# Expert weights by expert in 8 KB pieces, and the final norm's vector by a broadcast transfer

## The chip, the cores and the metric

The kernel runs on one core of one Trainium2 chip. The metric is the device time of one execution in microseconds (us). The engines are TensorE (PE in the profile; PEld is its weight loads), VectorE (DVE), ScalarE (ACT), GpSimd (POOL) and SyncE (SP), which here does little else than issue transfers. Sixteen DMA engines move data from HBM into SBUF.

## The reference

One layer on 256 tokens of 1024 features, float32. Stick-breaking attention and multi-scale retention run side by side on projections of the normed input, their outputs are merged by sigmoid gates, projected and added to the input. Then comes a mixture of 16 small experts:

```python
for e in range(N_EXPERTS):
    hidden = jax.nn.silu(xt @ w_exp_gate[e]) * (xt @ w_exp_up[e])
    y = y + combine[:, e:e + 1] * (hidden @ w_exp_down[e])
...
return rms_norm(h, norm_final_g)
```

Here `xt` is the normed residual, `combine` has two nonzero weights for each token (the best two experts of the token's best group), and the gate, up and down weights of an expert are 1024x512, 1024x512 and 512x1024: 6 MB in float32, 96 MB for all sixteen. The result is normed once more, with the vector `norm_final_g` of 1024 values.

## The kernel before, in words

**Slots.** SBUF is cut into 27 slots of 1 MB (128 partitions of 8 KB). `take` takes the slot that has been free for longest, `give` returns one. A list of loads, made once, holds every weight tile of the kernel in the order of use, each 1 MB. `pump` (its transfers are issued in L163) walks this list: as long as there is a free slot and a limit allows it, it takes the slot and has SP issue the tile's transfers. The code is written out in one order per engine; SP executes its issues in that order, and each waits until the last reader of the slot's old content is through. So a tile's load is issued when a slot is returned in the code, and starts when that slot's last product has run.

**Dense part** (up to about 245 us): the input is split into two rounded parts, every projection is three products (L281, L282, L284 and L294), and attention and retention are woven in between. The first expert tiles are loaded meanwhile.

**Routing and gather.** Tokens are ranked per expert; each expert has 64 places (`CAP`). `gather` (its products are in L945) multiplies 128 feature columns of the token rows `hn`, as the stationary operand, with a one-hot matrix and so makes `xgt[:, c, :]`: 128 features on the partitions, the places of eight experts on the columns. Which 128 features stand in block `c` is said by `features(c2, c)`: every second column of a stretch of 256. The scale of the norm, `fp`, is packed in the same order (`pack`).

**Experts**, in pairs i = 0 to 7, the two experts of a pair on the two halves of the output partitions. For each pair there is a gate step, an up step (both `proj`, L996) and a down step (L1032). A step has four rounds r = 0 to 3, and each of them uses one tile of 1 MB:
- A gate or up tile r (`plan_rows`) holds rows 256r to 256r + 255 of both experts. Partition p has rows 2p and 2p + 1 of each expert, so there are two transfers of 512 KB, and each partition's piece is 4 KB in a row. Round r multiplies blocks c = 2r and 2r + 1 with it and returns its slot (`after`).
- A down tile (`plan_down`) holds 256 rows of one expert; partition p has rows p and 128 + p, two pieces of 4 KB, in one transfer. The very last tile comes in two transfers.
- Between up and down, `hidden` (L1016) transposes the product of both, 128 columns at a time, with the identity as the moving operand; the scatter (L1050) adds a pair's output to the four accumulators `F`.

The order of steps is g0, u0, then for each i: g(i+1), d(i), u(i+1), with two exceptions: d3 comes ahead of g4, behind the gather of the second eight experts, and d6 comes behind u7. The loads stand in the same order. Written out, up(2) is the step u2.

**Two slots of the experts' phase aren't for weights.** `after` takes one as a work buffer at the end of round 0 of u0, and another at the end of round 1 of u0. Each takes the slot that would have gone to the next load.

**Final norm.** `final_gain` is called twice, ahead of round 2 of the last up step. It makes the vector `norm_final_g`, spread over 128 partitions, by eight transposes of one parameter column each, widened to 128 columns (L1168), and two copies on ACT (L1169). By then every load stands in SP's order already. `finish` runs the last scatter, sums squares on ACT (L1185), multiplies by the vector on DVE (L1186, its first reader) and writes the result.

If an expert gets more than 64 tokens, a branch runs the experts again; it isn't taken here.

Of the kernel before, what the change touches and what calls it, by code (L numbers as in the profile page):

```python
# [13 lines left out]
AF = mybir.ActivationFunctionType  # L14
# [3 lines left out]
P = 128  # L18
T = 256
D = 1024  # L20
KC = D // P
NB = T // P
# [52 lines left out]
R_FG = 32  # L75
R_BR = 40
R_WR = 60
R_GN = 220
R_FP = 228
R_N = 236  # L80


def pack(ins):
    w = np.concatenate([ins["w_group_router"][0], ins["w_expert_router"][0]], axis=1)
    b = np.concatenate([ins["b_group_router"][0], ins["b_expert_router"][0]])
    return np.ascontiguousarray(np.concatenate([
        ins["norm_mix_g"][0].reshape(KC, P).T,
        ins["b_gate"][0].reshape(16, P).T,
        ins["ret_norm_g"][0].reshape(8, P).T,
        ins["norm_ffn_g"][0].reshape(8, P).T,  # L90
        np.broadcast_to(b[None, :], (P, 20)),
        w.reshape(KC, P, 20).transpose(1, 0, 2).reshape(P, 160),
        ins["norm_final_g"].reshape(8, P).T,
        ins["norm_ffn_g"][0].reshape(4, P, 2).transpose(1, 0, 2).reshape(P, 8),
    ], axis=1))


@with_exitstack
def layer(ctx: ExitStack, tc, cst, dec, prm, x, w_in, w_gate, w_sb_out, w_ret_out,
          w_out, w_exp_gate, w_exp_up, w_exp_down, out):  # L100
    nc = tc.nc
    pe, act, dve, pool, sp = nc.tensor, nc.scalar, nc.vector, nc.gpsimd, nc.sync
# [17 lines left out]
    def take(shape=(P, 2048), dt=F32):  # L120
        s = free.pop(0)
        uid[0] += 1
        t = big.tile(list(shape), dt, name=f"b{uid[0]}", tag=f"s{s}")
        held[id(t)] = (s, t)
        return t
# [5 lines left out]
    def small(shape, dt=F32, name=None, bufs=1, tag=None):  # L131
        uid[0] += 1
        return sm.tile(list(shape), dt, name=f"{name}_{uid[0]}", tag=tag or name, bufs=bufs)

    def bank(name="d", dt=F32):
        uid[0] += 1
        return pp[name].tile([P, 512 if dt == F32 else 1024], dt, name=f"p{uid[0]}", tag=name)
# [7 lines left out]
    raws = {}  # L145
# [5 lines left out]
    def rows(w, r0, nk, c0, n):  # L151
        return w[r0:r0 + nk * P, c0:c0 + n].rearrange("(kc p) n -> p kc n", p=P)

    def plan(key, shape, parts, hook=None):
        loads.append((key, shape, parts, hook))

    def pump():
        while loads and loaded[0] < limit[0] and free:
            key, shape, parts, hook = loads.pop(0)
            t = raws[key] = take(shape)  # L160
            loaded[0] += 1
            for i, (at, src) in enumerate(parts):
                sp.dma_start(t[at], src)  # L163
                if hook:
                    hook(i)
# [6 lines left out]
    def drop(key):  # L172
        give(raws.pop(key))


    par = small([P, R_N], F32, "par")
    act.dma_start(par, prm)
# [15 lines left out]
    ident = cw[:, 2048 - P:2048]  # L193
# [4 lines left out]
    ident = identr.bitcast(F32)  # L198
# [259 lines left out]

    def plan_rows(which, w, i):
        for r in range(4):  # L460
            e = [w[0, 2 * i + j][256 * r:256 * r + 256].rearrange("(p k) n -> p k n", k=2) for j in range(2)]
            plan((which, i, r), [P, 2, 2, 512], [((slice(None), j), e[j]) for j in range(2)])

    def plan_down(i):
        for r in range(4):
            e = rows(w_exp_down[0, 2 * i + r // 2], 256 * (r % 2), 2, 0, D)
            cut = (i, r) == (NP - 1, 3)
            plan(("d", i, r), [P, 2, D],
                 [((slice(None), k), e[:, k]) for k in range(2)] if cut else [(slice(None), e)])
# [11 lines left out]
    for which, i in STEPS:  # L481
        if which == "d":
            plan_down(i)
        else:
            plan_rows(which, w_exp_gate if which == "g" else w_exp_up, i)
# [3 lines left out]
    key, shape, parts, hook = loads[2]  # L489
# [253 lines left out]
    i = 0  # L743
# [138 lines left out]
    xgt = take([P, KC, T])  # L882
# [46 lines left out]

    fp = par[:, R_FP:R_FP + 8]  # L930
    cm = small([P, NB, NP, 3], F32, "cm")
    cmb = small([P, NB, NP, 3, 3], BF16, "cmb")
    y2, work, gs = [], {}, {}

    def features(c2, c):
        return slice(256 * c2 + c, 256 * c2 + 256, 2)

    def gather(k, pt, cs=range(4)):

        for c2 in cs:  # L940
            ps = bank("m").rearrange("p (c s) -> p c s", c=2)
            for tb in range(NB):
                for h in range(2):
                    for c in range(2):
                        pe.matmul(ps[:, c, :], hn[h][:, tb, features(c2, c)], pt[tb].rearrange("p e s -> p (e s)"),  # L945
                                  start=c == 0 and tb == 0 and h == 0, stop=c == 1 and tb == 1 and h == 1,
                                  skip_group_check=True)
            tt(xgt[:, 2 * c2:2 * c2 + 2, :], ps,
               fp[:, 2 * c2:2 * c2 + 2][:, :, None].to_broadcast([P, 2, 2 * P]), op=ALU.mult)
# [23 lines left out]

    def after(key):
        drop(key)
        if not work and key == ("u", 0, 0):
            w = take([P, 2048])
            work.update(b=w[:, 0:512], ht=[w[:, 512 + 512 * k:1024 + 512 * k].rearrange("p (f s) -> p f s", f=4)
                                           for k in range(2)],
                        pb=w[:, 1536:1664].bitcast(BF16))  # L980
        if not y2 and key == ("u", 0, 1):
            w = take([P, 2048], F32R)
            y2.append(w[:, 0:1024].rearrange("p (h n) -> p h n", h=2))
            work["S"] = [w[:, 1024 + T * k:1024 + T * k + T] for k in range(2)]
        pump()

    def proj(i, which, ps, hook):
        o = 64 * (i % 4)
        for r in range(4):
            if hook:  # L990
                hook(r)
            w = raws[(which, i, r)]
            for k in range(2):
                c = 2 * r + k
                for j in range(2):
                    pe.matmul(ps[64 * j:64 * j + 64, :], xgt[:, c, o:o + 64], w[:, j, k, :],  # L996
                              start=c == 0, stop=c == KC - 1)
            after((which, i, r))

    def gate(i, hook=None):  # L1000
        g = bank("g")
        proj(i, "g", g, hook)
        return g
# [4 lines left out]
    def up(i, hook=None):  # L1008
        u = bank("g")
        proj(i, "u", u, hook)  # L1010
        stt(work["b"], u, gs[i][:, 0:1], work["b"], op0=ALU.mult, op1=ALU.mult)  # L1011

    def hidden(i):
        hps = bank("m").rearrange("p (f s) -> p f s", f=4)
        for f in range(4):
            pe.transpose(hps[:, f, :], work["b"][:, f * P:(f + 1) * P], ident)  # L1016
        act.activation(work["ht"][i % 2], hps, AF.Copy)  # L1017

    def down(i, hook=None):

        ht = work["ht"][i % 2]
        ys = [(bank(b), cs) for b, cs in zip("gm", pieces(i))]
        for r in range(4):
            if hook:
                hook(r)
            w = raws[("d", i, r)]
            j = r // 2
            for y, cs in ys:
                for k in range(2):
                    f = 2 * (r % 2) + k  # L1030
                    for q in range(2):
                        pe.matmul(y[64 * q:64 * q + 64, cs], ht[:, f, 64 * j:64 * j + 64],  # L1032
                                  w[:, k, 512 * q + cs.start:512 * q + cs.stop],
                                  start=r == 0 and k == 0, stop=r == 3 and k == 1)
            after(("d", i, r))
        for y, cs in ys:
            hilo(y2[0][:, 0, cs], y2[0][:, 1, cs], y[:, cs])
# [107 lines left out]
    def tail():  # L1145
        i = NP - 1

        def in_first(r):
            if r == 2:
                hidden(i)  # L1150

        def in_second(r):
            if r == 1:
                scatter(i - 1)

        down(i - 1, in_first)
        down(i, in_second)

    final = []

    def final_gain(q):
        if len(final) < 2:
            if not final:
                final.append(take([P, 2048])[:, 0:D])
            ps = bank("m")
            for k in range(4):
                c = R_GN + 4 * q + k
                pe.transpose(ps[:, k * P:(k + 1) * P], par[:, c:c + 1].to_broadcast([P, P]), ident)  # L1168
            act.activation(final[0][:, 512 * q:512 * q + 512], ps, AF.Copy)  # L1169
            if q == 1:  # L1170
                final.append(take([P, NB, D]))

    halves = [slice(0, 512), slice(512, D)]

# [66 lines left out]
```

## Time and profile before

| | us |
|---|---|
| median of 3 runs (lowest, highest) | 460.0 (459.87, 460.77) |
| the profiled execution | 460.21 |
| its span, first to last instruction | 458.5 |
| PE busy | 440.3 (96%) |
| DVE busy | 186.7 (41%) |
| ACT busy | 166.7 (36%) |

The granted clock of TensorE was 0.994 of full speed. The profile counts 58037 DMA packets with 142.49 MB, 311 GB/s over the span. In its chain of work that ended last, PE has 90% and DMA 4%.

How to read it: times in all views are us from the span's start, those marked ns excepted. The slices cut the span into 40 parts of 11.46 us; a digit is the busy share in tenths. The chain is followed back from the last instruction, at each step to what released it. A wait for several semaphores is put down to the one that came last by the profile, and can belong to another. Ends of matmuls are modelled.

### The profile page before, as it was taken

How to read it: one execution, taken by the hardware profiler on the slowest of the kernel's cores; microseconds unless marked ns; L12 is line 12 of the kernel's file. 1: busy time of each engine (PE TensorE's matmuls, PEld its weight loads, DVE VectorE, ACT ScalarE, POOL GpSimd, SP SyncE). 2: the span in 40 equal slices, each digit the busy share in tenths (PEclk: the TensorE clock that was granted, in tenths of full speed). 3: DMA queues.
4: the chain of work that ended last, by engine and by line, in shares of the span. 5: the costliest groups of instructions: out<-in, count | busy, mean ns of one | idle time of the engine just before them, and what ended most of it. 6: DMA issues, size and time to landing. Idle time of an engine off the chain costs nothing.

```text
span 458.5 us, 6741 instructions
## 1 busy us (share of the span) xinstructions
PE 440.3 (96%) x2715; PEld 297.7 (65%) x2715; DVE 186.7 (41%) x349; ACT 166.7 (36%) x246; POOL 22.1 (5%) x36
## 2 busy tenths in 40 slices
PE   7899999999999999999999999999989999999991
PEld 6699878887899999999998433333343333333340
DVE  4756488654357865678646420101022010101003
ACT  3543687894663655344534021010100010101103
POOL 2400110100002200000001000000000000000000
PEclk9999999999999999999999999999999999999997
DMA  8999998239402179995958989999999999999972
GB/s 280 353 381 387 393 356 272 91 95 315 140 1 93 39 240 394 408 390 186 362 188 291 338 306 411 408 410 410 408 409 410 408 409 408 410 407 410 410 302 98
DMA packets 58037, 142.49 MB, mean 311 GB/s; under 512 B 3344, under 2 KB 23952, under 8 KB 57872
## 3 DMA queue, kind: packets, MB, share of 16 engines
q1 hardware_dynamic: 57568, 141.35, 82.5%
q10 hardware_dynamic: 432, 0.65, 0.4%
q8 instruction: 23, 0.38, 0.3%
q14 instruction: 14, 0.11, 0.1%
HBM read 140.93 MB, written 1.05 MB: 310 GB/s over the span
## 4 chain that ended last, share of the span: by engine, by line
PE 90%; DMA 4%; DVE 2%; ACT 1%; issue 1%; POOL 1%; SPq 0%; ACTq 0%; DVEq 0%
PE p L996 25%; PE p L294 20%; PE p L1032 9%; PE p L281 8%; PE p L284 8%; PE p L282 8%; DMA b<-in_w_exp_down 3%; PE p L945 2%; PE p L1050 2%; PE z L586 1%; DMA b<-in_x 1%; PE p L1016 1%; PE p L688 1%; PE p L629 1%; PE z L617 1%
## 5 line engine op out<-in xcount | busy, mean ns | idle before, releaser
L253 DVE TENSOR_TENSOR b<-b,b 128x1024 fp32r<-128x1024 f32 x72 | 88.7, 1240 | 71.8 <-ACT b L251 70.7
L996 PE MATMUL p<-b,b 128*64 128x512 f32 x512 | 115.1, 596 | 0.0
L294 PE MATMUL p<-b,b 128*128 128x512 f32 (+1 forms) x504 | 102.4, 359 | 1.1 <-ACT b L251 0.9
L251 ACT ACTIVATE b<-b 128x1024 fp32r<-128x1024 f32 x72 | 75.5, 1056 | 76.7 <-PE p L282 47.8
L294 PEld LDWEIGHTS p<-b,b 128*128 128x128 f32 x504 | 82.3, 189 | 15.2 <-ACT b L251 1.3
L996 PEld LDWEIGHTS p<-b,b 128*64 128x64 f32 x512 | 35.1, 137 | 66.6 <-issue 63.8
L281 PE MATMUL p<-b,b 128*128 128x256 f32 x288 | 71.6, 286 | 0.0
L282 PE MATMUL p<-b,b 128*128 128x256 f32 x288 | 70.8, 283 | 0.0
L1032 PE MATMUL p<-b,b 128*64 128x512 f32 (+1 forms) x288 | 57.5, 547 | 0.9 <-ACT b L572 0.7
L281 PEld LDWEIGHTS p<-b,b 128*128 128x128 f32 x288 | 55.2, 192 | 0.5
L282 PEld LDWEIGHTS p<-b,b 128*128 128x128 f32 x288 | 55.2, 192 | 0.0
L1032 PEld LDWEIGHTS p<-b,b 128*64 128x64 f32 x288 | 20.2, 137 | 36.0 <-issue 31.5
L284 PE MATMUL p<-b,b 128*128 128x256 f32 x288 | 41.1, 283 | 0.0
L573 DVE SCALAR_TENSOR_TENSOR b<-p,b 128x512 fp32r<-128x512 f32 (+1 forms) x13 | 7.3, 565 | 81.0 <-ACT b L572 81.0
L284 PEld LDWEIGHTS p<-b,b 128*128 128x128 f32 x288 | 37.5, 192 | 0.0
L1011 DVE SCALAR_TENSOR_TENSOR b<-p,share,b 128x512 f32<-128x512 f32 x8 | 6.0, 751 | 60.3 <-PE p L996 60.3
L972 ACT ACTIVATE b<-p 128x256 fp32r<-128x256 bf16 x8 | 3.1, 383 | 75.5 <-PE p L971 75.5
L572 ACT ACTIVATE b<-p 128x512 fp32r<-128x512 f32 (+1 forms) x13 | 6.4, 495 | 52.9 <-PE p L1032 52.2
L1006 ACT ACTIVATE b<-p,share 128x512 f32<-128x512 f32 x8 | 5.5, 687 | 21.2 <-PE p L996 21.2
L1017 ACT ACTIVATE b<-p 128x512 f32<-128x512 f32 x8 | 4.8, 597 | 20.7 <-PE p L1016 20.7
L945 PEld LDWEIGHTS p<-pt,b 128*128 128x128 f32 x64 | 8.1, 195 | 4.4 <-DVE pt L863 2.3
L1188 POOL TENSOR_TENSOR rf<-rf,mhalf 128x1 f32<-128x1 f32 x2 | 1.1, 540 | 203.4 <-DVE rf L1187 203.4
(169 smaller groups left out, 329.4 us busy)
## 6 DMA issues: line engine op xcount, KB each, us to landing
b<-in_w_exp_gate SPq DMA_DIRECT2D x64, 512.0 KB, 10.2
b<-in_w_exp_up SPq DMA_DIRECT2D x64, 512.0 KB, 10.2
b<-in_w_exp_down SPq DMA_DIRECT2D x31, 1024.0 KB, 12.7
b<-in_w_in SPq DMA_DIRECT2D x17, 1024.0 KB, 14.3
b<-in_w_gate SPq DMA_DIRECT2D x8, 1024.0 KB, 10.4
b<-in_w_ret_out SPq DMA_DIRECT2D x4, 1024.0 KB, 8.7
b<-in_w_out SPq DMA_DIRECT2D x4, 1024.0 KB, 6.4
b<-in_w_sb_out SPq DMA_DIRECT2D x2, 1024.0 KB, 5.1
```

The lines of the kernel that those rows point to most:

```text
L251: act.activation(hi, raw, AF.Copy)
L253: tt(lo, raw, hi.bitcast(F32), op=ALU.subtract)
L281: pe.matmul(ps, wh[:, k, cs], h[:, k, :], start=k == 0, stop=False)
L282: pe.matmul(ps, wh[:, k, cs], l[:, k, :], start=False, stop=False)
L284: pe.matmul(ps, wl[:, k, cs], h[:, k, :], start=False, stop=k == nk - 1)
L294: pe.matmul(ps[tb], kth(a, k)[:, tb * P:(tb + 1) * P], b[:, j, :], start=n == 0 and k == 0, stop=n == 2 and k == KC - 1)
L572: act.activation(hi, src, AF.Copy)
L573: stt(lo, src, 1.0, hi.bitcast(F32), op0=ALU.mult, op1=ALU.subtract)
L945: pe.matmul(ps[:, c, :], hn[h][:, tb, features(c2, c)], pt[tb].rearrange("p e s -> p (e s)"), start=c == 0 and tb == 0 and h == 0, stop=c ...
L996: pe.matmul(ps[64 * j:64 * j + 64, :], xgt[:, c, o:o + 64], w[:, j, k, :], start=c == 0, stop=c == KC - 1)
L1032: pe.matmul(y[64 * q:64 * q + 64, cs], ht[:, f, 64 * j:64 * j + 64], w[:, k, 512 * q + cs.start:512 * q + cs.stop], start=r == 0 and k == ...
L1050: pe.matmul(F[q][tb][:, cs], work["S"][i % 2][r, tb * P:(tb + 1) * P], y2[0][r, h, cs], start=False, stop=last and h == 1 and cs.stop == 5 ...
```

## The change

Four things:
- A gate or up tile holds 512 rows of one expert instead of 256 rows of both: tile r has expert r % 2, rows 512 (r // 2) on, partition p rows 4p to 4p + 3. It is one transfer of 1 MB with 8 KB in a row for each partition. Rounds 0 and 1 each read both of the first two tiles, rounds 2 and 3 both of the last two, and the slots are returned two at a time, behind rounds 1 and 3.
- A down tile has rows 2p and 2p + 1 on partition p, 8 KB in a row. The very last still comes in two transfers, of 4 KB pieces.
- The order of features follows: block c takes every fourth column of a stretch of 512 (`features`), `fp` is packed for it, and `hidden` transposes every second column of a stretch of 256.
- `final_gain` takes a slot and has SP issue one transfer that reads the vector's 4 KB for each of 128 partitions; the eight transposes and two copies go, and so do eight columns of the parameter table. The work buffer is taken at the end of round 3 of g0.

```diff
--- before.py
+++ after.py
@@ -75,9 +75,8 @@
 R_FG = 32
 R_BR = 40
 R_WR = 60
-R_GN = 220
-R_FP = 228
-R_N = 236
+R_FP = 220
+R_N = 228
 
 
 def pack(ins):
@@ -90,13 +89,12 @@
         ins["norm_ffn_g"][0].reshape(8, P).T,
         np.broadcast_to(b[None, :], (P, 20)),
         w.reshape(KC, P, 20).transpose(1, 0, 2).reshape(P, 160),
-        ins["norm_final_g"].reshape(8, P).T,
-        ins["norm_ffn_g"][0].reshape(4, P, 2).transpose(1, 0, 2).reshape(P, 8),
+        ins["norm_ffn_g"][0].reshape(2, P, 4).transpose(1, 0, 2).reshape(P, 8),
     ], axis=1))
 
 
 @with_exitstack
-def layer(ctx: ExitStack, tc, cst, dec, prm, x, w_in, w_gate, w_sb_out, w_ret_out,
+def layer(ctx: ExitStack, tc, cst, dec, prm, gfr, x, w_in, w_gate, w_sb_out, w_ret_out,
           w_out, w_exp_gate, w_exp_up, w_exp_down, out):
     nc = tc.nc
     pe, act, dve, pool, sp = nc.tensor, nc.scalar, nc.vector, nc.gpsimd, nc.sync
@@ -458,12 +456,12 @@
 
     def plan_rows(which, w, i):
         for r in range(4):
-            e = [w[0, 2 * i + j][256 * r:256 * r + 256].rearrange("(p k) n -> p k n", k=2) for j in range(2)]
-            plan((which, i, r), [P, 2, 2, 512], [((slice(None), j), e[j]) for j in range(2)])
+            e = w[0, 2 * i + r % 2][512 * (r // 2):512 * (r // 2) + 512].rearrange("(p k) n -> p k n", k=4)
+            plan((which, i, r), [P, 4, 512], [(slice(None), e)])
 
     def plan_down(i):
         for r in range(4):
-            e = rows(w_exp_down[0, 2 * i + r // 2], 256 * (r % 2), 2, 0, D)
+            e = w_exp_down[0, 2 * i + r // 2][256 * (r % 2):256 * (r % 2) + 256].rearrange("(p k) n -> p k n", k=2)
             cut = (i, r) == (NP - 1, 3)
             plan(("d", i, r), [P, 2, D],
                  [((slice(None), k), e[:, k]) for k in range(2)] if cut else [(slice(None), e)])
@@ -933,7 +931,7 @@
     y2, work, gs = [], {}, {}
 
     def features(c2, c):
-        return slice(256 * c2 + c, 256 * c2 + 256, 2)
+        return slice(512 * (c2 // 2) + 2 * (c2 % 2) + c, 512 * (c2 // 2) + 512, 4)
 
     def gather(k, pt, cs=range(4)):
 
@@ -973,7 +971,7 @@
 
     def after(key):
         drop(key)
-        if not work and key == ("u", 0, 0):
+        if not work and key == ("g", 0, 3):
             w = take([P, 2048])
             work.update(b=w[:, 0:512], ht=[w[:, 512 + 512 * k:1024 + 512 * k].rearrange("p (f s) -> p f s", f=4)
                                            for k in range(2)],
@@ -989,13 +987,15 @@
         for r in range(4):
             if hook:
                 hook(r)
-            w = raws[(which, i, r)]
+            w = [raws[(which, i, r // 2 * 2 + j)] for j in range(2)]
             for k in range(2):
                 c = 2 * r + k
                 for j in range(2):
-                    pe.matmul(ps[64 * j:64 * j + 64, :], xgt[:, c, o:o + 64], w[:, j, k, :],
+                    pe.matmul(ps[64 * j:64 * j + 64, :], xgt[:, c, o:o + 64], w[j][:, c % 4, :],
                               start=c == 0, stop=c == KC - 1)
-            after((which, i, r))
+            if r % 2:
+                after((which, i, r - 1))
+                after((which, i, r))
 
     def gate(i, hook=None):
         g = bank("g")
@@ -1013,7 +1013,8 @@
     def hidden(i):
         hps = bank("m").rearrange("p (f s) -> p f s", f=4)
         for f in range(4):
-            pe.transpose(hps[:, f, :], work["b"][:, f * P:(f + 1) * P], ident)
+            o = 256 * (f // 2) + f % 2
+            pe.transpose(hps[:, f, :], work["b"][:, o:256 * (f // 2) + 256:2], ident)
         act.activation(work["ht"][i % 2], hps, AF.Copy)
 
     def down(i, hook=None):
@@ -1159,16 +1160,11 @@
     final = []
 
     def final_gain(q):
-        if len(final) < 2:
-            if not final:
-                final.append(take([P, 2048])[:, 0:D])
-            ps = bank("m")
-            for k in range(4):
-                c = R_GN + 4 * q + k
-                pe.transpose(ps[:, k * P:(k + 1) * P], par[:, c:c + 1].to_broadcast([P, P]), ident)
-            act.activation(final[0][:, 512 * q:512 * q + 512], ps, AF.Copy)
-            if q == 1:
-                final.append(take([P, NB, D]))
+        if not final:
+            final.append(take([P, 2048])[:, 0:D])
+            sp.dma_start(final[0], gfr.to_broadcast([P, D]))
+        elif len(final) < 2:
+            final.append(take([P, NB, D]))
 
     halves = [slice(0, 512), slice(512, D)]
 
@@ -1228,7 +1224,7 @@
 
     ins = {k: np.ascontiguousarray(v) for k, v in inputs.items()}
     cst, dec = constants()
-    feed = {"cst": cst, "dec": dec, "prm": pack(ins)}
+    feed = {"cst": cst, "dec": dec, "prm": pack(ins), "gfr": ins["norm_final_g"].reshape(1, D)}
     feed.update({f"in_{k}": ins[k] for k in _INS})
     nc = _bacc.Bacc("TRN2", target_bir_lowering=False, num_devices=1, dynamic_dma_scratch_size=1024)
     args = [nc.dram_tensor(k, a.shape, mybir.dt.from_np(a.dtype), kind="ExternalInput").ap()
```

## Rows read from the trace of the kernel before

**Rows 1.** The slices of the page: PE, DMA, and what DMA moved.
```profile
PE   7899999999999999999999999999989999999991
...
DMA  8999998239402179995958989999999999999972
GB/s 280 353 381 387 393 356 272 91 95 315 140 1 93 39 240 394 408 390 186 362 188 291 338 306 411 408 410 410 408 409 410 408 409 408 410 407 410 410 302 98
```

**Rows 2.** The chain that ended last, 427 to 459: start, length, what.
```profile
430.02 15.67 DMA b<-in_w_exp_down
...
445.73 1.51 PE p L1032 x12
```

**Rows 3.** Waits, 429 to 448: engine, line, releaser, us in total, times, longest.
```profile
PEld p L1032 <- DMA b<-in_w_exp_down: 2.0, 3, 0.9
PE p L1032 <- ACT b L572: 0.7, 1, 0.7
```

**Rows 4.** The chain, 276 to 430.
```profile
277.43 6.87 PE p L1032 x32
...
371.22 0.66 PE p L1016 x4
...
408.84 1.13 PE p L1050 x8
...
425.06 1.02 PE p L1168 x8
426.08 3.61 PE p L996 x16
```

**Rows 5.** Windows: stretch, length, engines' busy time, clock, DMA share, GB/s last.
```profile
40.00:44.00 4.00, 4.00 (x36) 4.00 (x35) 1.97 (x3) 1.74 (x2) 0.00 (x0) 1.00 1.05 385
45.00:50.00 5.00, 5.00 (x32) 4.07 (x32) 2.13 (x4) 2.17 (x3) 0.00 (x0) 1.00 1.04 406
264.00:268.00 4.00, 4.00 (x24) 1.32 (x22) 0.81 (x5) 2.16 (x3) 0.00 (x0) 1.00 0.68 266
268.00:276.00 8.00, 7.87 (x44) 2.72 (x42) 1.62 (x6) 1.17 (x3) 0.00 (x0) 1.00 0.91 331
280.00:435.00 155.00, 152.87 (x761) 55.73 (x756) 18.08 (x49) 15.27 (x27) 0.00 (x0) 1.00 1.03 409
```

**Rows 6.** Waits of SP's queue, 262 to 275.
```profile
SPq L163 <- PE p L996: 7.6, 3, 5.9
```

**Rows 7.** Timeline of SP, single issues: start, length, line, what.
```profile
267.68 0.34 SPq L163 DMA_DIRECT2D b<-in_w_exp_up  x1
...
269.40 0.33 SPq L163 DMA_DIRECT2D b<-in_w_exp_up  x1
...
415.08 0.33 SPq L163 DMA_DIRECT2D b<-in_w_exp_up  x1
```

**Rows 8.** The chain, 249 to 275: rounds of up(0) and gate(1).
```profile
261.92 3.58 PE p L996 x16
...
265.77 7.02 PE p L996 x32
```

**Rows 9.** DMA, 45 to 50: packets by size.
```profile
DMA packets 641, 2.03 MB, mean 406 GB/s; under 512 B 32, under 2 KB 32, under 8 KB 514
```

**Rows 10.** DMA issues, 405 to 416: count, KB each, median us to landing.
```profile
b<-in_w_exp_up SPq DMA_DIRECT2D x8, 512.0 KB, 10.5
```

**Rows 11.** Timeline of DVE, 445 to 452: the vector's first reader.
```profile
449.33 0.69 DVE L1186 TENSOR_TENSOR b<-p,b 128x512 f32<-128x512 f32 x1 [1.19 <-ACT b L1185]
```

**Rows 12.** Weight loads by line, 245 to 459 (L281: 20:45): busy us, mean ns.
```profile
L996 PEld LDWEIGHTS p<-b,b 128*64 128x64 f32 x512 | 35.1, 137 | 66.6 <-issue 63.8 <-DMA b<-in_w_exp_gate 0.9 <-DMA b<-in_w_exp_up 0.7
...
L945 PEld LDWEIGHTS p<-pt,b 128*128 128x128 f32 x64 | 8.1, 195 | 4.4 <-DVE pt L863 2.3 <-issue 1.6 <-DVE b L948 0.5
...
L1016 PEld LDWEIGHTS p<-identr,b 128*128 128x128 f32 x32 | 3.4, 141 | 2.6 <-DVE share L965 1.8 <-issue 0.8
...
L281 PEld LDWEIGHTS p<-b,b 128*128 128x128 f32 x64 | 12.3, 192 | 0.0
```

## The prediction

> **What bounds the kernel now.** I read the slices first [rows 1]: TensorE (PE) is full nearly throughout, and from slice 25 to slice 38 the DMA engines are full too, at about 410 GB/s. So two chains run side by side through the experts, and only the end says which one sets the time. The chain that ended last [rows 2] says it: the last piece of the last down tile lands 15.67 us after its issue, at 445.69; the last 12 products start at 445.73, run 1.51 us, and the scatter and the final norm follow, which depend on nothing else. The waits of that stretch [rows 3] show PE's weight loads held three times by down tiles, 2.0 us in all, and 0.7 us put down to ScalarE. It is the only weight transfer on this chain from 405 on.
>
> So the expert loads are the bound, but only just. PE's own pace for what stands behind the last up products (they end at 426.08 + 3.61 = 429.69 [rows 4]): 6.87 us for a down step (x32), 0.66 for the hidden transposes, another 6.87 (the last step has twice the products at half the width), 1.13 for a scatter [rows 4]: 15.53, so PE alone would be through at 445.2; it was through at 445.73 + 1.51 = 447.24 [rows 2]. The 2.04 us between agree with the 2.0 of [rows 3].
>
> Where the load chain begins is seen in the windows [rows 5]: 409 GB/s from 280 to 435, but 266 and 331 from 264 to 268 and 268 to 276. There SyncE (SP) waits for PE to free a slot [rows 6]: 7.6 us in three waits. From about 276 on it has always something queued. The end of the loads is thus the moment at which the first load behind that idle stretch is issued, plus the service time of all behind it.
>
> **Pairs (later frees).** Before, each product round r of a gate or up step frees its tile. Now rounds 0 and 1 read the same two tiles and free them together at the end of round 1; 2 and 3 likewise. The first load behind the idle stretch is the first tile of up(2). Its slot now is that of up(0)'s third tile, free when round 2 of up(0) ended: issue 267.68 [rows 7]. After the change this slot is free when round 3 ends; the trace has an issue at that moment, the next one, 269.40. That is 1.72 us later. The tile before it (fourth of down(1)) moves too, to the end of round 1 of up(0), 261.92 + 3.58 = 265.50 [rows 8]; 3.9 us ahead of that issue, more than its own 2.5 us of transfer, so it doesn't push on. Later pairs matter less: gate(1)'s first pair is free at 265.77 + 7.02 = 272.79 [rows 8], before up(2)'s first two tiles are through. From 268 to 276 DMA lost 8 x (409 - 331)/409 = 1.5 us, of which some 1.1 lies ahead of up(2)'s data; the other 0.4 is regained, since both loads of a pair are then queued. Bounds: 1.3 (all regained) to 2.3 (a 1 MB transfer starts 0.5 later than a half one). I take **+1.8 us** on the end of the loads.
>
> **8 KB packets.** Behind up(2)'s first tile come 67 tiles of 1 MB; at 409 GB/s [rows 5] each takes 1.0486/0.409 = 2.564 us. How fast are 8 KB packets? In 40 to 44 the loads are of 2 KB and run at 385; at 16 engines that is 85.1 ns a packet, and 4 KB at 409 is 160.2 ns: 75.1 ns per further 2 KB. By this line 8 KB take 310.4 ns, or 422 GB/s. The trace has such packets: of the 641 between 45 and 50, 514 are under 8 KB, so 127 are of 8 KB (the table of decays, 1.04 MB) [rows 9]. The stretch moved 406 x 5 = 2030 KB; the other 990 at 385 take 2.57 us, the 1040 KB took 2.43: 427 GB/s. Bounds: 409 (no gain) and 427 (2.456 us a tile, 7.2 us over 67 tiles). I take 420, below the line: 2.497 us, 0.066 a tile, **-4.4 us**. With +1.8 the last tile lands 2.6 us earlier, at 443.1, and the products behind it end at 447.24 - 2.6 = 444.64.
>
> The Trainium skill (DMA: Bandwidth & Descriptors, "Why small descriptors are slow (HBM only)") gives three bus cycles per packet beside one for every 32 bytes: 131 cycles for 4 KB, 259 for 8. That is only 1.1% a byte; the line through 385 and 409 gives 3.2%. By the page the loads would gain some 2 us, not 4.4.
>
> **One transfer a tile.** Eight 512 KB transfers took 10.5 us to land [rows 10], at 409 GB/s about 8 x 0.524 MB: eight are in flight. Eight of 1 MB only deepen the queue: 0. SP issues half as many. That a round needs two tiles: the last half of up(7) was issued at 415.08 [rows 7] and landed near 425.6; round 2 began at 426.08. Now, with most of the 2.6 us gained, it lands near 423.5 and PE is there at 425.06, 1.5 us later: 0. If the loads were late here, PE would only wait sooner for what it waits for anyway.
>
> **The final norm's vector.** Eight products with the identity and their gap go: 1.02 us of PE at 425.06 [rows 4]. Its copies on ScalarE are off the path. This is hidden in the forecast: PE alone would end at 445.2 - 1.02 = 444.2, and the loads let it end at 444.64. It becomes the floor: no gain is over 447.24 - 444.2 = 3.04 us. If the 0.7 us wait on ScalarE in [rows 3] is real and no masked load, the floor is 444.9 and the gain 2.34. In its place 512 KB come on SP's queue, issued behind the last weights, so they delay none: 1.28 us at 409, there at 444.4. Its first reader is VectorE at 449.33 [rows 11], then 446.7: 2.3 us to spare. Bounds: 0, and 128 packets one after another at 160 ns, since all read the same 4 KB: 20.5 us. I take 0, as the stream in front of it has the same packet size and count per engine.
>
> **Strides.** The gather's 64 weight loads now step over 16 bytes, not 8; the 32 hidden transposes step over 8, not 4. The 8-byte step cost nothing so far: 195 ns against 192 for contiguous columns [rows 12]. A 16-byte step no row shows. Bounds: 0, and twice the column time: 128 columns take 195, 64 take 137 [rows 12], so 116 ns per load, 7.4 us in all. The transposes load at 141; at most 195 - 141 = 54 ns each, 1.7 us. I take 0 for both, by the row for the 8-byte step. The work buffer taken at the end of gate(0), and a parameter table of 8 columns less: 0; the one is first written a round later, the other is read long after it lands.
>
> **Sum.** Span 458.5, 460.21 with what lies around it: 460.21 - 2.6 = 457.6. The runs' median is 460.0, 0.2 lower, so I forecast **457.5**.
>
> **Rivals.**
> *A, bytes alone count.* The rate stays 409; then only the pairs' +1.8 is left: 462.0, slower. For it: 409 is held flat for 155 us, as at a ceiling. Against: 427 in the stretch with 8 KB. It decides if the gain per tile is under 1.8/67 = 0.027 us (413 GB/s).
> *B, half the gain.* Rows of 2 and 4 KB don't say how a third size goes; at 414 GB/s, half of what 420 gives, 2.2 us stand against 1.8: 459.8, no change that can be measured (a measurement of this kernel tells 0.2%, or 0.9 us, from none). For it: 385 and 409 are near each other, and the next doubling can only give less. Against: 427. The skill's packet cost above comes out here.
> *C, the 16-byte step.* If each of the 64 loads takes 116 ns more, half of it (3.7 us) comes ahead of up(0)'s frees and moves the loads as well, and PE's own end is 444.2 + 7.4 = 451.6: 460.2 + 4.4 = 464.6. It decides from 0.45 us on, where PE's own pace takes over. For it: no row has the step. Against: the step from 4 to 8 bytes shows no trend. The Trainium skill (SBUF — State Buffer, the note "SBUF cachelines" under "Door 1") has lines of 16 bytes and asks for at least two hits in one for full rate; an 8-byte step has two, in agreement with the 195 ns, a 16-byte step has one.
> *D, the vector comes late.* If 128 reads of one row run one after another it lands at 463.6, 16.9 us after its reader: 474.5; at half of that cost about 464. It decides from 3.6 us on (146 GB/s).
>
> **Chances.** Forecast 0.64 (its own range 456.9 to 459.0, by the floor and by 415 GB/s), A 0.08, B 0.12, C 0.10, D 0.06. Range: 456.9 to 462.1, with A and B in it. Faster by over 0.2% 0.66 (the forecast, and a weak D), within 0.2% 0.15 (B, and a weak C), slower 0.19.
>
> **What the next profile would show.** DMA at 418 to 425 GB/s from 280 on (409: A). Idle DMA near 265 to 271, up(2)'s first issue at about 269.4, and the last landing near 443.1. The gather's weight loads at 195 ns and its x16 at 2.19 us (C: over 250 ns and 4 us). The broadcast landing before 446. Waits for down tiles at the end of about 0.5 us instead of 2.0. I am wrong if the rate is up and the end is not earlier, or if PE waits for gate or up tiles.

## The result and the profile after

The changed kernel takes 465.58 us (median of 4 runs, 465.14 to 466.62) beside 460.25 for the kernel before on the same chip: a ratio of 1.0113, 95% interval 1.0101 to 1.0126. It is 5.3 us slower, where 2.5 us faster was forecast (457.5 from a median of 460.0), and the time lies outside the range of 456.9 to 462.1. The profiled execution took 465.14 us, its span is 463.3.

The slices first, of what DMA did (they answer to [rows 1]):

```profile
DMA  8999998249202289995948579999999999999942
GB/s 276 353 382 391 390 355 258 85 140 314 88 1 92 93 250 420 417 351 185 362 142 328 194 306 419 424 419 424 419 422 423 421 420 420 422 424 417 422 182 96
```

The transfers are faster than before in every full slice, at about 421 GB/s. Seen from the end of the kernel they are also through earlier: the last slice but one shows 182 GB/s instead of 302. The windows of the changed kernel (columns as in [rows 5]) say the same of the rate, and show DMA part idle ahead of it:

```profile
256.00:264.00 8.00, 8.00 (x37) 4.31 (x36) 3.71 (x16) 0.00 (x0) 0.00 (x0) 1.00 0.47 187
264.00:272.00 8.00, 8.00 (x40) 2.58 (x38) 0.97 (x5) 2.35 (x3) 0.00 (x0) 1.00 0.79 288
...
280.00:440.00 160.00, 158.14 (x760) 60.36 (x756) 18.09 (x49) 14.29 (x25) 0.00 (x0) 0.99 1.01 421
```

SP's issues around that stretch, and the last load's issue with its time to landing (answering to [rows 7]):

```profile
268.82 0.33 SPq L161 DMA_DIRECT2D b<-in_w_exp_down  x1
...
272.67 0.33 SPq L161 DMA_DIRECT2D b<-in_w_exp_up  x1
...
428.55 0.33 SPq L161 DMA_DIRECT2D b<-in_w_exp_down  x1
```
```profile
L161 SPq DMA_DIRECT2D b<-in_w_exp_down x1: 328/328/328, 428.6 to 428.6; - x1
...
DMA to landing us min/median/max: 17.4/17.4/17.4
```

The first load of up(2) is issued at 272.67, not at the forecast 269.4, and yet the last weights have landed at 428.55 + 17.4 = 445.95, hardly later than the 445.69 of [rows 2]. The end of the kernel is no longer theirs. The chain at the end (answering to [rows 2]):

```profile
436.13 3.43 PE p L1033 x16
439.57 0.68 PE p L1017 x4
...
446.69 5.33 PE p L1033 x48
452.02 1.37 PE p L1051 x14
```

It is PE without a gap; no wait for a down tile is left of the 2.0 us in [rows 3]. The products behind the last load end at 452.02 instead of 447.24: 4.78 us later, which is the span's 4.8. So PE lost time further up. The place is the gather. The chain of the changed kernel there, and then the weight loads by line (they answer to [rows 12]) and the products by line (busy us, mean ns):

```profile
249.07 4.01 PE p L943 x16
253.08 1.87 PE p L994 x8
254.95 2.07 PE p L943 x8
...
343.38 4.12 PE p L943 x16
```
```profile
L943 PEld LDWEIGHTS p<-pt,b 128*128 128x128 f32 x64 | 15.4, 329 | 4.3 <-DVE pt L861 2.3 <-issue 1.6 <-DVE b L946 0.3
...
L1017 PEld LDWEIGHTS p<-identr,b 128*128 128x128 f32 x32 | 4.7, 209 | 2.6 <-DVE share L963 1.8 <-issue 0.8
```
```profile
L943 PE MATMUL p<-pt,b 128*128 128x256 f32 x64 | 16.5, 412 | 1.3 <-DVE pt L861 1.2
...
L1017 PE MATMUL p<-identr,b 128*128 128x128 f32 x32 | 6.3, 322 | 0.8
```

And the gather's products in the kernel before:

```profile
L945 PE MATMUL p<-pt,b 128*128 128x256 f32 x64 | 9.1, 291 | 1.6 <-DVE pt L863 1.2 <-DVE b L948 0.3
```

A weight load of the gather takes 329 ns instead of 195, and its 64 products hold PE for 16.5 us instead of 9.1: 7.4 us. Half of it lies ahead of up(0), whose rounds free the slots, so up(2)'s first issue comes 272.67 - 267.68 = 5.0 us later: 1.7 by the pairs, 3.6 by the first half of the gather, less the 0.34 by which the gather began earlier (249.07, before 249.41).

The sum of PE's side: its own end was 445.2; 7.4 for the gather, 0.6 for the hidden transposes (0.74 instead of 0.66 for each of eight), less 1.02 for the products that went, less the 0.34 of the gather's start: 451.8, against 452.02 in the trace.

The granted clock of TensorE is lower as well, 0.988 of full speed over the run instead of 0.994. One stretch of that lies in the second gather. After 1.2 us of idling and some 2.6 us of the gather's products the clock fell from 1.00 to 0.50, its 1.2 GHz level, from 346 to 348, and was 0.65 from 348 to 350. This is not where the time went: the second gather's products took 4.12 + 3.96 = 8.08 us on the chain, the first's, at 1.00, took 4.01 + 2.07 + 2.07 = 8.15. Only the four transposes between them took 0.85 instead of 0.74.

### The profile page after: what moved, and what is told of

It reads as the page before. It is cut to its first block, busy times and chain, and to the rows that moved or that the text cites. A ratio compares the mean times of both kernels' runs of the same rounds, so it can differ in the third digit from the quotient of the medians.

```text
span 463.3 us, 6655 instructions
## 1 busy us (share of the span) xinstructions
PE 446.5 (96%) x2707; PEld 305.2 (66%) x2707; DVE 187.1 (40%) x349; ACT 165.7 (36%) x244; POOL 22.4 (5%) x36
## 4 chain that ended last, share of the span: by engine, by line
PE 93%; DVE 2%; ACT 1%; issue 1%; DMA 1%; POOL 1%; ACTq 0%; DVEq 0%
PE p L994 24%; PE p L292 19%; PE p L1033 12%; PE p L279 8%; PE p L282 7%; PE p L280 7%; PE p L943 4%; PE p L1051 2%; PE z L584 1%; PE p L1017 1%; DMA b<-in_x 1%; PE p L686 1%; PE p L627 1%; PE z L615 1%; PE p L829 1%
## 5 line engine op out<-in xcount | busy, mean ns | idle before, releaser
L943 PEld LDWEIGHTS p<-pt,b 128*128 128x128 f32 x64 | 15.4, 329 | 4.3 <-DVE pt L861 2.3
L943 PE MATMUL p<-pt,b 128*128 128x256 f32 x64 | 16.5, 412 | 1.3 <-DVE pt L861 1.2
```

## Experiments

Theory 1: the 16-byte step of the gather's weight loads made the kernel slower, and everything else went as forecast. Theory 2: the paired frees did it. Ratios are to the kernel before in the same set of runs, with their 95% interval.

**e1: the step alone.** The kernel before with

```diff
-        return slice(256 * c2 + c, 256 * c2 + 256, 2)
+        return slice(512 * (c2 // 2) + 2 * (c2 % 2) + c, 512 * (c2 // 2) + 512, 4)
```

and `fp` packed for it.

> The kernel before with one edit: the gather's 64 weight loads step over 16 bytes instead of 8 (the weights' rows are not reordered to match, so the output is another function). Theory 1, the step is what made the changed kernel slower: weight loads about 329 ns instead of 195, 7.4 us more of TensorE in two halves; TensorE's own end 445.2 + 7.4 = 452.6, the last load 3.6 later at 449.3 and so covered; time 460.2 + 5.4 = 465.6, with no wait for down tiles. Theory 2, the paired frees made it slower and the step only shows as longer records: same time as before, 460.2 within 0.5.

465.96 us beside 460.40, ratio 1.0131 (1.0116 to 1.0146). Its weight loads by line, and its chain at the end:

```profile
L945 PEld LDWEIGHTS p<-pt,b 128*128 128x128 f32 x64 | 15.4, 330 | 4.2 <-DVE pt L863 2.3 <-issue 1.6 <-DVE b L948 0.3
```
```profile
447.00 5.33 PE p L1032 x48
452.33 1.38 PE p L1050 x12
```

Forecast were 465.6, 329 ns and an end of the products at 452.6; no wait for a down tile is left. The step alone costs as much as the whole change. (Its gather began at 248.83, 0.58 ahead of the kernel before; by that the forecast would have been 452.0.)

**e2: the pairs alone.** The kernel before, tiles by expert, 4 KB pieces, and the work buffer taken as in the change. Of its edit, the lines that make the pairs:

```diff
+            e = w[0, 2 * i + r % 2][512 * (r // 2):512 * (r // 2) + 512].rearrange("(a p k) n -> p a k n", a=2, k=2)
+            plan((which, i, r), [P, 2, 2, 512], [((slice(None), a), e[:, a]) for a in range(2)])
...
+            if r % 2:
+                after((which, i, r - 1))
+                after((which, i, r))
```

> The kernel before with tiles by expert and paired frees, pieces still 4 KB, the gather still at 8 bytes. Theory 1: only the forecast's +1.8 us on the end of the loads: 462.0, first load of up(2) issued at about 269.4, DMA 409 GB/s, the wait for down tiles at the end some 3.8 us. Theory 2: the pairs carry the loss, 465 or more, TensorE waits for gate or up tiles.

461.94 us beside 460.40, ratio 1.0043 (1.0026 to 1.0059): 1.5 us, where 1.8 was forecast. SP, then the waits and the chain at the end:

```profile
268.54 3.76 SPq L163 DMA_DIRECT2D b<-in_w_exp_up  x5
```
```profile
PEld p L1034 <- DMA b<-in_w_exp_down: 4.0, 4, 1.5
PE p L1034 <- DMA b<-in_w_exp_down: 1.4, 3, 0.6
```
```profile
431.25 15.68 DMA b<-in_w_exp_down
...
446.97 1.51 PE p L1034 x12
```

up(2)'s first load is issued at 268.54, not at the expected 269.4, but the gather began earlier too, at 248.57: from there it is 19.97 us, before 18.27, so the pairs cost 1.70 as forecast. The loads still end the kernel, 1.24 us later than in [rows 2]; the waits grew, and no step waits for gate or up tiles. Theory 2 is out.

**e3: the changed kernel with gate and up pieces of 4 KB**, so that the gather is back at 8 bytes; pairs, down tiles and broadcast stay (tiles as in e2).

> The changed kernel with gate and up pieces back at 4 KB, two rows in a row, so that the gather steps over 8 bytes again; pairs, broadcast and 8 KB down tiles stay. Theory 1: weight loads at 195 ns; of the 67 tiles behind the idle stretch 24 are down tiles and gain 0.066 each, 1.6 us, against 1.8 for the pairs: end of the loads +0.2, time 460.4 (459.9 to 461.0). Theory 2: no better than the changed kernel, 465.

460.24 beside 460.40, ratio 1.0003 (0.9995 to 1.0012). Weight loads 197 ns and 413 GB/s from 280 to 435:

```profile
L943 PEld LDWEIGHTS p<-pt,b 128*128 128x128 f32 x64 | 8.1, 197 | 4.3 <-DVE pt L861 2.3 <-issue 1.6 <-DVE b L946 0.4
```
```profile
280.00:435.00 155.00, 152.92 (x754) 55.95 (x750) 18.09 (x49) 14.20 (x25) 0.00 (x0) 1.00 1.02 413
```

What the down tiles gain, the pairs take, as forecast; without the 16-byte step the loss is gone.

**e4: the changed kernel with `hn` in block order**, so that the gather's columns are contiguous:

```diff
...
+        hi, lo = [t[:, tb, 512 * g:512 * g + 512].rearrange("p (k q) -> p k q", k=4)[:, :, p0:p0 + 64] for t in
+                  (hn + hn[:1])[:2]]
+        v = xt[:, tb, wo_cols[n]].rearrange("p (q k) -> p k q", k=4)
...
+        return slice(128 * (2 * c2 + c), 128 * (2 * c2 + c) + 128)
```

`rows_onto` reads it back in the old order.

> The changed kernel with the rows hn stored in block order, so that the gather's 128 weight columns are contiguous; all transfers as in the changed kernel. The copies that write hn read with a step of 16 bytes and the eight residual products read their moving operand with a step of 512 bytes. Theory 1: gather at 192 to 195 ns, loads at 421 GB/s, last weights near 443; TensorE's own end 444.2 plus 0.6 for the hidden transposes (209 ns instead of 141): 457.9, or up to 459.5 if the eight products cost double. Theory 2 (pairs): 464 to 465.

458.58 beside 460.40, ratio 0.9968 (0.9955 to 0.9980): faster than both kernels. Weight loads, ScalarE's copy, the rate, the start of the gather and the chain's end:

```profile
L948 PEld LDWEIGHTS p<-pt,b 128*128 128x128 f32 x64 | 7.9, 189 | 4.3 <-DVE pt L865 2.3 <-issue 1.6 <-DVE b L951 0.4
L1022 PEld LDWEIGHTS p<-identr,b 128*128 128x128 f32 x32 | 4.4, 207 | 2.7 <-DVE share L968 1.8 <-issue 0.8
```
```profile
L441 ACT ACTIVATE b<-b 128x256 fp32r<-128x256 f32 x8 | 5.0, 667 | 1.7 <-DVE b L837 1.7
```
```profile
280.00:435.00 155.00, 152.94 (x754) 56.11 (x752) 18.09 (x49) 14.19 (x25) 0.00 (x0) 1.00 1.01 421
```
```profile
249.96 2.23 PE p L948 x16
```
```profile
440.19 5.33 PE p L1038 x48
445.52 1.37 PE p L1056 x14
```

The last weights land at 443.2 (issued at 425.5, 17.7 us to landing), where the prediction had 443.1. The products end at 445.52, against the prediction's 444.64. PE bounds it: 0.6 more for the transposes, and a gather that starts at 249.96, 0.55 late. That the slower copies cause the late start is likely but not shown: in kernels with the old copies the gather started anywhere from 248.57 (e2) to 249.72 (e3).

**e5: the broadcast alone**, the kernel before with the change's `final_gain`.

> The kernel before with the broadcast transfer in place of the eight transposes, nothing else. Theory 1 (the loads end the kernel, TensorE's 1.02 us lie behind them): same time, 460.3 within 0.5; waits for down tiles grow from 2.0 to about 3 us; the vector lands some 2 us behind the last weights, ahead of its reader. Theory 2 (the products counted): 1.0 us faster, 459.4. Theory 3 (128 reads of one row are slow): slower, the reader waits for the transfer.

460.30 beside 460.22, ratio 0.9996 (0.9988 to 1.0005): nothing, as theory 1 had it. The waits and the chain's end:

```profile
PEld p L1030 <- DMA b<-in_w_exp_down: 2.5, 4, 1.1
```
```profile
430.01 15.75 DMA b<-in_w_exp_down
...
445.81 1.52 PE p L1030 x12
```

**e6: down tiles alone in 8 KB pieces**, the kernel before with the change's `plan_down` and `hidden`.

> The kernel before with down tiles in 8 KB pieces, and so the hidden transposes over 8 bytes; gate and up, frees and final vector as before. Theory 1: 24 of the 67 last tiles at 421 instead of 409 GB/s, 0.073 us each: the loads end 1.75 us earlier, products behind them at 445.5; TensorE's own end 445.2 + 0.6 for the slower transposes = 445.8 bounds it: 1.4 us faster, 459.0. Theory 2 (a transfer's rate does not matter so near to TensorE's own pace): 460.4 or slower by the 0.6.

459.32 beside 460.22, ratio 0.9977 (0.9969 to 0.9986): 0.9 us, of 1.4 forecast. DMA moved 414 GB/s from 280 to 435. The end of the products, which PE now bounds (446.03, where 445.8 was expected; no wait for a down tile is left):

```profile
440.69 5.33 PE p L1033 x48
446.03 1.38 PE p L1051 x12
```

**e7 and e8: other steps in the gather**, 3 columns (12 bytes) and 8 columns (32 bytes); one run each.

> The kernel before with the gather's weight loads over 12 bytes, three columns (the features are then the wrong ones and some are used twice: another function). If any second hit in 16 bytes is what counts, four columns lie in three lines and the load is between 195 and 329 ns, near 295. If only a step of 16 bytes or more costs, 195.

> The same with a step of 32 bytes (again another function). If each column costs one line, the same 329 ns and 250 ns a product as at 16 bytes, time 465.6. If distance itself costs, more: about 600 ns.

460.99 and 466.84 us; e7's single time lies within the runs of the kernel before (459.5 to 461.25), so only its trace tells something. Their weight loads (ns: least, median, most), e7 first:

```profile
L945 PEld LDWEIGHTS p<-pt,b x64: 251/260/263, 248.7 to 347.2; 128*128 128x128 f32 x64
```
```profile
L945 PEld LDWEIGHTS p<-pt,b x64: 312/338/345, 249.0 to 352.9; 128*128 128x128 f32 x64
```

So 12 bytes are not free, and distance counts little beyond 16: 195, 260, 330, 338 ns for 8, 12, 16 and 32 bytes. The gather's 64 products hold PE for 9.1, 12.5, 16.5 and 17.0 us.

**e9 to e12: e4's two leftovers.** e9 turns the copies round (read in order, write with a step of 512 bytes); e10 and e11 store the gated product in block order, so that the hidden transposes read contiguous columns; e12 is e9 with e11.

```diff
-        stt(work["b"], u, gs[i][:, 0:1], work["b"], op0=ALU.mult, op1=ALU.mult)
+        b = work["b"].rearrange("p (h k q) -> p h k q", h=2, k=2)
+        v = u.rearrange("p (h q k) -> p h k q", h=2, k=2)
+        for h in range(2):
+            stt(b[:, h], v[:, h], gs[i][:, 0:1], b[:, h], op0=ALU.mult, op1=ALU.mult)
```

That is e11; e10 has both views in the order `p h q k`. Silu is written the same way.

> e4 with the copies that write hn turned round: they read the residual in order and write with a step of 512 bytes, instead of reading with a step of 16 and writing in order (in e4 they took 667 ns on ScalarE and 615 on VectorE for 256 columns, before 412 and 418). Theory 1, a read pays by the 16-byte line and a write does not: 412 and 418 ns again, the gather starts at about 249.3 instead of 249.96, time 0.6 us under e4: 458.0. Theory 2, a write pays as much for each line: same as e4, 458.6, or up to 0.5 worse.

458.43, ratio 0.9962 (0.9948 to 0.9976). The copies are no shorter (theory 2), and yet this gather starts at 249.59, 0.37 ahead of e4's:

```profile
L441 ACT ACTIVATE b<-b 128x256 fp32r<-128x256 f32 x8 | 4.7, 662 | 1.8 <-DVE b L837 1.8
```

> e4 with the gated product stored in block order, so that the 32 hidden transposes read contiguous columns: silu and product read PSUM in order and write with a step of 512 bytes (the product in two instructions). Theory 1, the transposes pay by the line: weight loads 141 ns instead of 207, 0.08 us a step, 0.6 in all, TensorE bounds e4, so 458.0. Theory 2, what the copies cost comes back behind the second gather, where the product is on the path: 458.6 or worse.

> The same with the other order: silu and product read PSUM with a step of 8 bytes and write in order. Same gain on TensorE, 458.0, if PSUM reads at 8 bytes cost nothing; if they cost, the copies are longer than in e10 (687 ns silu and 751 ns product before).

458.45 and 458.32, ratios 0.9955 (0.9940 to 0.9971) and 0.9950 (0.9934 to 0.9967). First e10, silu and product; then e11, with its transposes' weight loads:

```profile
L1011 ACT ACTIVATE b<-p,share 128x512 f32<-128x512 f32 x8 | 9.4, 1176 | 21.7 <-PE p L999 21.7
L1020 DVE SCALAR_TENSOR_TENSOR b<-p,share,b 128x256 f32<-128x256 f32 x16 | 9.4, 663 | 59.7 <-PE p L999 59.7
```
```profile
L1025 PEld LDWEIGHTS p<-identr,b 128*128 128x128 f32 x32 | 3.4, 140 | 2.7 <-DVE share L968 1.8 <-issue 0.8
```
```profile
L1020 DVE SCALAR_TENSOR_TENSOR b<-p,share,b 128x256 f32<-128x256 f32 x16 | 7.0, 480 | 59.7 <-PE p L999 59.7
L1011 ACT ACTIVATE b<-p,share 128x512 f32<-128x512 f32 x8 | 5.5, 688 | 21.7 <-PE p L999 21.7
```

The transposes are back at 140 ns in both. Writes with the wide step cost (1176 ns for silu, 687 in order), reads of PSUM at 8 bytes don't (688).

> e9 and e11 together: hn written in block order by a step of 512 bytes, the gated product stored in block order and read from PSUM with a step of 8 bytes; everything else as in the changed kernel. TensorE bounds both: 0.4 us of e9's earlier gather and 0.4 of e11's cheaper transposes should add, 458.0, and no wait for down tiles. If the loads bound it now, it stays at 458.3 and waits for down tiles show.

458.32, ratio 0.9956 (0.9943 to 0.9970). In its trace the terms add (products end at 444.54, 0.98 ahead of e4, and no wait for a down tile), but the traced execution took 457.60, the lowest of its five. The medians of e4, e9, e10, e11 and e12, 458.3 to 458.6, are not told apart by their intervals, and the 458.0 that stood for a gain in each of e9 to e12 was missed by 0.3 to 0.45:

```profile
439.21 5.33 PE p L1041 x48
444.54 1.38 PE p L1059 x14
```

## Why the prediction was wrong

The step that failed is **Strides**: "I take 0 for both, by the row for the 8-byte step." The runs show 7.4 us in its place for the gather, which is the upper bound given there, and 0.6 for the transposes; e1 shows that the gather's step alone makes the loss. This is rival C, to which I gave 0.10, with its place, its price, its signs (over 250 ns and 4 us: 329 and 4.01) and nearly its time: 464.6 forecast, 465.58 measured. The prediction's own sign of being wrong came in too: the rate is up and the end is not earlier. What was wrong was the choice between two bounds far apart. The row I leaned on was at 8 bytes, and it could not carry the 16: its load is flat from 4 to 8 bytes, but the transposes' quicker loads rise there already (141 to 209 ns). That fits a slower stage that hid the step in the gather's loads; which one, no run shows. A flat row says nothing of the next step. The other bound, from 64 columns in 137 ns and 128 in 195 [rows 12], gave 116 ns a load, and the gather paid 7.4 us over 64 products, 116 each. So close a match is luck in part: the bound was meant for the length of a load, and that grew by 134. The Trainium skill (SBUF — State Buffer, the note "SBUF cachelines" under "Door 1") had the rule that spoke against the change: at least two hits in a line of 16 bytes for full rate. The traces agree for the gather (195 ns at two hits, 330 at one) and not for the transposes (209 ns at two hits, 141 at four); I had it at 0.10.

The other terms, one by one:
- Pairs, +1.8: e2 has +1.5. In the changed kernel the issue moved by 5.0, since half of the gather sits ahead of the frees as well; C had said so.
- 8 KB packets, 420 GB/s: 421 measured. It lies at the line through 2 and 4 KB (422) and below the 427 that the 127 packets of [rows 9] gave; the rates of rivals A (409) and B (414) are out. By the Trainium skill's three bus cycles a packet (DMA: Bandwidth & Descriptors, "Why small descriptors are slow (HBM only)") a byte would take an estimated 1.1% less time; from 409 to 421 it takes 2.9% less, and the measurement decides.
- The eight products: hidden as forecast, e5 shows 0. In the changed kernel, where PE is the bound, their 1.02 us do count: from the gather's start to the end of the products e1, which has them and the old transposes, takes 203.50 us, the changed kernel 202.95. That is 0.55 less, where 1.02 - 0.6 = 0.4 is the sum.
- The broadcast: it was issued at 431.08 and landed 16.1 us later, at 447.2, 1.2 us behind the last weights. Its first reader ran at 454.10. Rival D is out.

```profile
L1165 SPq DMA_DIRECT2D b<-gfr x1: 327/327/327, 431.1 to 431.1; - x1
...
DMA to landing us min/median/max: 16.1/16.1/16.1
```
```profile
454.10 0.69 DVE L1182 TENSOR_TENSOR b<-p,b 128x512 f32<-128x512 f32 x1 [1.19 <-ACT b L1181]
```

- The transposes: 209 ns instead of 141, above the 195 that I had as their bound. A step of four costs 0.08 us more, not 4 x 68 ns: 0.6 in all.

With the gather's step removed (e4) the loads do what was forecast (443.2 for 443.1), but it is PE and not the loads that ends the kernel: 458.58 measured, 457.5 forecast. PE's floor of 444.2 with 0.6 for the transposes and 0.55 for the late gather makes 445.35, of the 445.52 in the trace.

## What to carry to other kernels

When transfers and TensorE end within two microseconds of each other, a change of layout that helps the one can be paid for by the other, as here: follow a new order of rows to every place that reads it with a stride. Where a stride is new, take its cost from its bounds, not from a smaller stride that was free. If larger pieces are wanted, reorder the stationary operand once, when it is written, instead of at each read (e4).

## What the runs showed of the hardware

- In these runs a weight load pays by the 16-byte line, a stretch of 16 bytes that it touches. The gather's 128 columns touch 32, 64, 96, 128 and 128 lines at steps of 4, 8, 12, 16 and 32 bytes, and take 189, 195, 260, 330 and 338 ns: from 64 lines on 2.1 ns a line ((330 - 195)/64). The transposes' loads, quicker at 32 lines (141 ns), pay it from there: 209 ns at 64 lines, again 2.1 a line.
- The slower clock did not lengthen these loads: ten of the gather's loads between 345.8 and 349 in the changed kernel, at a granted clock of 0.50 to 0.65, took 330 ns, those of the first gather at 1.00 took 328.
- Copies pay too: 256 columns took 412 ns on ScalarE and 418 on VectorE, 667 and 615 when read with a step of 16 bytes. Turning it round, writing with a step of 512 bytes, cost the same (662 on ScalarE).
- Reading PSUM with a step of 8 bytes cost ScalarE nothing (688 ns for 512 columns, 687 in order).
- Transfers in 8 KB pieces ran at 421 GB/s, in 4 KB pieces at 409. 128 reads of the same 4 KB did not hold up: they landed 1.2 us behind the stream ahead of them, and 512 KB at 409 take 1.28.
